# Four-block weight chunks, the residual parked in DRAM, and four seven-product units in every block of gate and up

## The chip, the core and the metric

The kernel runs on one core of one Trainium2 chip. The metric is the device time of one execution in microseconds. TensorE (PE) multiplies, VectorE (DVE) and ScalarE (ACT) prepare its operands, GpSimd (POOL) does a few small operations, and SyncE (SP) issues nearly all loads.

## The reference

One decoder layer for 256 tokens of width 2048, in float32:

```python
f1 = swiglu(rms_norm(h, ffn1_pre_norm), ffn1_w_gate, ffn1_w_up, ffn1_w_down)   # 2048 -> 5504 -> 2048
h = h + 0.5 * rms_norm(f1, ffn1_post_norm)
m = hybrid_token_mixer(rms_norm(h, mix_pre_norm), ...)
h = h + rms_norm(m, mix_post_norm)
f2 = swiglu(rms_norm(h, ffn2_pre_norm), ffn2_w_gate, ffn2_w_up, ffn2_w_down)
h = h + 0.5 * rms_norm(f2, ffn2_post_norm)

def swiglu(x, w_gate, w_up, w_down):
    return (jax.nn.silu(x @ w_gate) * (x @ w_up)) @ w_down
```

The mixer projects its input by `w_in` (2048 to 11280 columns), runs two causal linear attentions with gates (GLA with 4 heads, HGRN2 with 8), multiplies each by a branch matrix, gates and adds the two, and multiplies by `w_out`.

## The kernel before

**Products of split operands.** Each float32 operand is split into a high part (rounded by an ACT copy, `hi`) and a low part (a DVE subtraction, `lo`). A product of two operands is three matmuls (`mm3`, lines 155 to 159): high by high, low by high, high by low. The tokens stand in two tiles of 128 (`t`), and a block of weights has 128 rows and 512 columns (`CB`).

**Plain units and units with seven products.** Gate and up are computed together, one block of 512 columns of each (`gemm_pair`, line 329), into four accumulators `c[t][i]`: two token tiles by two matrices. A unit `u` is two blocks of rows of both matrices, that is four blocks of weights. A plain unit has eight products. A unit with seven products (`Blocks.seven`, line 265, called "a seven" below) uses a Strassen-like scheme: DVE adds blocks of weights to each other, four of the seven products go to shared accumulators `p1`, `p5`, `p6`, `p7`, and three straight to `c`. At the end of the block of columns `share` forms sums of the four and `close` adds them to `c`. It needs sums of the left operand too, made once (`operand_sums`, line 208). `SUMS` gives three units of eight the seven products, `FOUR` gives four. In the FFNs every second block of columns has `FOUR`, and the others have `SUMS`; the first block has none. In the mixer most pairs of columns have `SUMS`. `down_proj` has sevens too, six in each half of its output columns.

**Weights on their way.** SP loads a chunk of two blocks (128x1024 elements) into a `raw` buffer; ACT copies the high part to `whi`; DVE subtracts to get `wlo`. `raw`, `whi` and `wlo` have five buffers each (`RING`). A seven takes two raw buffers and two of each part. The sums of its weights and their high and low parts lie in three tiles of 128x1536 from the pool `rows`, which has three buffers in all (`row_tile`, line 379) that the shared sums and other row tiles use too. A buffer is reused when all that used it before has ended.

**Order.** The order of units in a block of columns is written out in `gemm_pair` (lines 346 to 354). Other work (transposes, attention) is spread between them by `Side`: its `pump` makes a step at each unit. Where `late` is set, in five pairs of columns of the mixer, the sevens come behind the first plain units, with half a plain unit between two sevens, so that attention has the front of the block. The tools that build the program fix the order on each engine beforehand, where an instruction can go ahead of an earlier one that still waits.

**The residual** `h` (2 MB) stays in SBUF through both FFNs; in the mixer it is stored to DRAM (`away`) and its tiles hold other things.

Of the kernel before, what the change touches and what calls it, by code (L numbers as in the profile page):

```python
# [15 lines left out]
P = 128  # L16
# [11 lines left out]
RW = 2 * CB  # L28
STEPS = ((3, 2, 2, 2), (6, 1, 1, 1))
RING = 5  # L30
AHEAD = 3
# [55 lines left out]
def kernel(ctx: ExitStack, tc: tile.TileContext, a: dict, out: bass.AP):  # L87
# [22 lines left out]
    h = [[hpool.tile([P, CB], F32, name=f"h{t}_{n}") for n in range(4)] for t in range(NT)]  # L110

    away = [[dram.tile([P, CB], F32, name=f"away{t}_{n}") for n in range(4)] for t in range(NT)]
# [10 lines left out]

    def ring_alloc(w):
        hi, lo = [ring.tile([P, RW], F32R, tag=s, name=nm(s))[:, :2 * w]
                  .rearrange("p (i c) -> p i c", i=2) for s in ("whi", "wlo")]
        return [(hi, lo)]

    def wload(src: bass.AP, w: int, apart=False):
        raw = ring.tile([P, RW], F32, tag="raw", name=nm("raw"))[:, :2 * w].rearrange(  # L130
            "p (i c) -> p i c", i=2)
        for i in range(2) if apart else [slice(0, 2)]:
            nc.sync.dma_start(raw[:, i, :], src[:, i, :])
        return raw, apart

    def wchunk(src: bass.AP, w: int, alloc=ring_alloc, raw=None):


        raw, apart = raw or wload(src, w)
        parts = alloc(w)  # L140
        if len(parts) == 1:
            hi, lo = parts[0]
            for i in range(2) if apart else [slice(0, 2)]:
                split_into(hi[:, i, :], lo[:, i, :], raw[:, i, :])
            return [(hi[:, i, :], lo[:, i, :]) for i in range(2)]
        for i, (hi, lo) in enumerate(parts):
            split_into(hi, lo, raw[:, i, :])
        return parts
# [12 lines left out]
    def gemm_block(w_dram, c0, w, lhs, nkt=KT, held=None, raws=(), ready=()):  # L161
# [4 lines left out]
        raws, ready = list(raws), list(ready)  # L166
        nb = -(-w // CB)
        step = 2 // nb
        pss = [[ps_tile(f"mm{t}") for _ in range(nb)] for t in range(NT)]

        def chunk(k0, alloc):
            if ready:
                return ready.pop(0)
            raw = raws.pop(0) if raws else None
            src = w_dram[k0 * P:(k0 + step) * P, c0:c0 + w]
            return wchunk(src.rearrange("(k p) c -> p k c", p=P) if nb == 1 else
                          src.rearrange("p (n c) -> p n c", n=nb), w // nb, alloc, raw)

        def mm(t, k0, parts):
            for i, part in enumerate(parts):  # L180
                kt = k0 + i % step
                mm3(pss[t][i // step][:, :w // nb], lhs(t, kt), part, kt == 0, kt == nkt - 1)

        if held is None:
            for k0 in range(0, nkt, step):
                parts = chunk(k0, ring_alloc)
                for t in range(NT):
                    mm(t, k0, parts)
                side.pump()
        else:  # L190
            kept = []
            for i, k0 in enumerate(range(0, nkt, 2)):
                kept.append((k0, chunk(k0, ring_alloc if i < RING else held)))
                mm(0, *kept[-1])
                side.pump()
            for k in kept:
                mm(1, *k)
                side.pump()
            side.flush()
# [45 lines left out]
    class Blocks:  # L245
# [19 lines left out]
        def seven(self, u, end):  # L265
            w, k0 = self.w, 2 * u
            ra, rb = [ring.tile([P, RW], F32, tag="raw", name=nm("raw"))[:, :2 * w]
                      .rearrange("p (i c) -> p i c", i=2) for _ in range(2)]
            wsum, hi, lo = [row_tile(n, d)[:, :, :w] for n, d in
                            (("wsum", F32), ("wsumh", F32R), ("wsuml", F32R))]  # L270

            nc.sync.dma_start(ra[:, 0, :], self.block(0, k0))
            nc.sync.dma_start(ra[:, 1, :], self.block(1, k0 + 1))
            nc.sync.dma_start(rb[:, 0, :], self.block(1, k0))
            nc.sync.dma_start(rb[:, 1, :], self.block(0, k0 + 1))

            (ahi, alo), (bhi, blo) = ring_alloc(w) + ring_alloc(w)
            nc.scalar.activation(ahi, ra, AF.Copy)  # L278
            add(wsum[:, 0:2, :], ra, rb[:, 0:1, :].broadcast_to([P, 2, w]))
            nc.scalar.activation(hi[:, 0:2, :], wsum[:, 0:2, :], AF.Copy)  # L280
            add(rb[:, 0, :], wsum[:, 0, :], ra[:, 1, :])
            nc.scalar.activation(bhi, rb, AF.Copy)  # L282
            summed = add(wsum[:, 2, :], rb[:, 0, :], rb[:, 1, :])
            last[0] = nc.scalar.activation(hi[:, 2, :], wsum[:, 2, :], AF.Copy)  # L284
# [4 lines left out]
            first, second, third = [[(part[0][:, i, :], part[1][:, i, :]) for i in range(n)]  # L289
                                    for part, n in (((ahi, alo), 2), ((bhi, blo), 2), ((hi, lo), 3))]  # L290
# [3 lines left out]
            self.product("p1", self.lhs(0, k0), first[0], end)  # L294
            self.product((0, 1), self.part("s4", u), first[1])
            self.product((0, 0), self.lhs(0, k0 + 1), second[1])
            side.pump()
            self.product("p6", self.part("s2", u), second[0], end)
            self.product("p5", self.part("d", u), third[0], end)
            self.product("p7", self.part("s3", u), third[1], end)  # L300
            self.product((1, 0), self.lhs(1, k0 + 1), third[2])
# [21 lines left out]
    def first_of(w_dram, c0, w=CB):  # L323
        def chunk(i):
            return wchunk(w_dram[2 * i * P:2 * (i + 1) * P, c0:c0 + w]
                          .rearrange("(k p) c -> p k c", p=P), w)
        return chunk

    def gemm_pair(ws, w, lhs, sums, ready=(), following=(), raws=(), sevens=SUMS,
# [11 lines left out]
        def split(i, k0):  # L341
            return wchunk(None, w, raw=raws.pop(0)) if raws else first_of(*ws[i], w)(k0 // 2)

        steps = [(u, i) for u in range(nu) if u not in sevens for i in range(2)]
        if late:
            at = range(6, 6 + 2 * len(sevens), 2)
        elif len(sevens) > len(SUMS):
            at = range(3, 3 + 2 * len(sevens), 2)  # L350
        else:
            at = [2 * u - j for j, u in enumerate(sevens)]
        for j, u in zip(at, sevens):
            steps.insert(j, (u, None))
        ready = list(ready)
        for j, (u, i) in enumerate(steps):
            side.fast = late
            if any(i is None for _, i in steps[j:j + 2]):
                side.full = True
            if i is None:  # L360
# [3 lines left out]
            parts = ready.pop(0) if ready else split(i, k0)  # L364
            if (u, i) == (nu - 1, 0) and sevens:
                ready = [split(1, k0)]
                b.share()
            for t in range(NT):
                b.plain((k0, k0 + 1), t, i, parts, u == nu - 1)
            side.pump()  # L370
        ready = [chunk(0) for chunk in following]
# [162 lines left out]
    def out_proj(w_dram, nkt, lhs, post, scale, pre, homes, following):  # L534
# [8 lines left out]
        def load(kt, hf, alloc=ring_alloc):  # L543
            return wchunk(w_dram[kt * P:(kt + 1) * P, hf * 1024:(hf + 1) * 1024]
                          .rearrange("p (n c) -> p n c", n=2), CB, alloc)

        def mm(t, n, kt, parts):
            if acc[t][n] is None:
                acc[t][n] = ps_tile(f"acc{t}{n}")
            mm3(acc[t][n], lhs(t, kt), parts[n % 2], kt == 0, kt == nkt - 1)  # L550

        order = [(kt, hf) for hf in range(2) for kt in range(2)]
        order += [(kt, hf) for kt in range(2, nkt - TAIL) for hf in range(2)]
        for i, (kt, hf) in enumerate(order):
            parts = load(kt, hf)
            if 6 <= i < 10:
# [5 lines left out]
                load_bcast(wpost[-1], post, i - 6, last[0])  # L562
            for t in range(NT):
                for n in (2 * hf, 2 * hf + 1):
                    mm(t, n, kt, parts)
            if i == 1:
                side.flush()
        tail = [[(kt, load(kt, hf, homes[hf * TAIL + i]))
                 for i, kt in enumerate(range(nkt - TAIL, nkt))] for hf in range(2)]

        for t in range(NT):
            ss = small.tile([P, 4], F32, tag="ss", name=nm("ss"))
            for n in range(4):
                for i, (kt, parts) in enumerate(tail[n // 2]):
# [12 lines left out]
    def down_proj(w_dram, nkt, lhs, sums_of, post, pre, wpost, ys, homes, following):  # L587
# [8 lines left out]
        def split(hf, kt, alloc=ring_alloc):  # L596
            return wchunk(w_dram[kt * P:(kt + 1) * P, hf * 1024:(hf + 1) * 1024]
                          .rearrange("p (n c) -> p n c", n=2), CB, alloc)
# [18 lines left out]
        ahead = []  # L617
        for hf in range(2):
# [6 lines left out]
            kt = 0  # L625
            while kt < n:
                u = kt // 2
# [732 lines left out]
```

## Time and profile before

| | us |
|---|---|
| three runs | 2083.17, 2084.71, 2084.87 (median 2084.71) |
| span of the profiled execution | 2083.3 |
| PE, DVE, ACT, POOL busy | 2069.5, 1855.3, 1240.8, 40.7 |

The profile gives the span of its execution and no time beside it; the median of the runs is 1.4 us above that span. Busy time is counted while at least one instruction of the engine runs; matmuls overlap, so starts say more of their cost than durations do. The first FFN ends near 690 us and the second begins near 1400 us; the mixer lies between.

### The profile page before, as it was taken

How to read it: one execution, taken by the hardware profiler on the slowest of the kernel's cores; microseconds unless marked ns; L12 is line 12 of the kernel's file. 1: busy time of each engine (PE TensorE's matmuls, PEld its weight loads, DVE VectorE, ACT ScalarE, POOL GpSimd, SP SyncE). 2: the span in 40 equal slices, each digit the busy share in tenths (PEclk: the TensorE clock that was granted, in tenths of full speed). 3: DMA queues.
4: the chain of work that ended last, by engine and by line, in shares of the span. 5: the costliest groups of instructions: out<-in, count | busy, mean ns of one | idle time of the engine just before them, and what ended most of it. 6: DMA issues, size and time to landing. Idle time of an engine off the chain costs nothing.

```text
span 2083.3 us, 29324 instructions
## 1 busy us (share of the span) xinstructions
PE 2069.5 (99%) x10509; PEld 1722.0 (83%) x10509; DVE 1855.3 (89%) x2187; ACT 1240.8 (60%) x1670; POOL 40.7 (2%) x87
## 2 busy tenths in 40 slices
PE   9999999999999999999999999999999999999998
PEld 7888888898888888878888888888888888898886
DVE  7898999989899779989999897578999989999896
ACT  6555656566666575576655554465555655666663
POOL 1000000000000100000000000010000000000000
PEclk9999999999999999999999999999999999999999
DMA  8666656667767466555566566755665656576663
GB/s 267 184 209 201 213 187 197 210 185 223 216 191 235 148 201 210 159 172 188 178 195 195 178 220 216 221 182 171 222 197 188 207 187 225 164 238 202 202 206 128
DMA packets 200666, 412.24 MB, mean 198 GB/s; under 512 B 18036, under 2 KB 26423, under 8 KB 200520
## 3 DMA queue, kind: packets, MB, share of 16 engines
q1 hardware_dynamic: 194896, 401.80, 60.9%
q10 hardware_dynamic: 5624, 8.57, 1.4%
q8 instruction: 82, 1.34, 0.3%
q14 instruction: 64, 0.52, 0.1%
HBM read 406.11 MB, written 4.19 MB: 197 GB/s over the span
## 4 chain that ended last, share of the span: by engine, by line
PE 96%; ACT 2%; DVE 1%; issue 1%; DMA 0%; POOL 0%; SPq 0%; DVEq 0%; POOLq 0%; ACTq 0%
PE c L157 22%; PE c L159 21%; PE c L158 21%; PE p L159 5%; PE p L157 5%; PE p L158 5%; PE mm L157 3%; PE mm L159 3%; PE mm L158 3%; PE ps L397 2%; PE acc L157 1%; PE acc L158 1%; PE acc L159 1%; PE ps L905 0%; DVE h L510 0%
## 5 line engine op out<-in xcount | busy, mean ns | idle before, releaser
L151 ACT ACTIVATE whi<-raw 128x1024 fp32r<-128x1024 f32 (+3 forms) x498 | 511.0, 1033 | 284.8 <-PE c L158 116.8
L153 DVE TENSOR_TENSOR wlo<-raw,whi 128x1024 fp32r<-128x1024 f32 (+3 forms) x498 | 587.7, 1190 | 85.5 <-ACT whi L151 84.2
L157 PE MATMUL c<-whi,xhi 128*128 128x512 f32 (+1 forms) x1270 | 495.8, 391 | 0.1
L159 PE MATMUL c<-wlo,xhi 128*128 128x512 f32 (+1 forms) x1270 | 490.9, 387 | 0.0
L158 PE MATMUL c<-whi,xlo 128*128 128x512 f32 (+1 forms) x1270 | 490.6, 386 | 0.0
L243 DVE TENSOR_TENSOR wlo<-raw,whi 128x1024 fp32r<-128x1024 f32 (+1 forms) x252 | 294.5, 1202 | 12.2 <-ACT whi L278 6.1
L159 PEld LDWEIGHTS c<-wlo,xhi 128*128 128x128 f32 x1270 | 238.5, 188 | 47.5 <-DVE wlo L153 0.3
L157 PEld LDWEIGHTS c<-whi,xhi 128*128 128x128 f32 x1270 | 238.6, 188 | 46.3 <-ACT xhi L469 0.5
L158 PEld LDWEIGHTS c<-whi,xlo 128*128 128x128 f32 x1270 | 238.7, 188 | 45.0
L282 ACT ACTIVATE whi<-raw 128x1024 fp32r<-128x1024 f32 (+1 forms) x126 | 131.8, 1046 | 203.9 <-DVE raw L243 80.9
L243 DVE TENSOR_TENSOR wsuml<-wsum,wsumh 128x1536 fp32r<-128x1536 f32 (+1 forms) x126 | 218.1, 1731 | 36.8 <-ACT wsumh L284 36.5
L157 PE MATMUL c<-whi,hkhi 128*128 128x512 f32 x558 | 217.0, 389 | 0.0
L159 PE MATMUL c<-wlo,hkhi 128*128 128x512 f32 x558 | 216.8, 388 | 0.0
L158 PE MATMUL c<-whi,hklo 128*128 128x512 f32 x558 | 216.7, 388 | 0.0
L280 ACT ACTIVATE wsumh<-wsum 128x1024 fp32r<-128x1024 f32 (+1 forms) x126 | 131.6, 1045 | 107.4 <-DVE wsum L243 70.5
L278 ACT ACTIVATE whi<-raw 128x1024 fp32r<-128x1024 f32 (+1 forms) x126 | 131.6, 1044 | 103.0 <-PE c L158 87.7
L243 DVE TENSOR_TENSOR wsum<-raw,raw 128x1024 f32<-128x1024 f32 (+1 forms) x126 | 151.8, 1205 | 21.6 <-DMA raw<-in_ffn_w_down_dram 18.1
L159 PEld LDWEIGHTS c<-wlo,hkhi 128*128 128x128 f32 x558 | 104.7, 188 | 21.6
L158 PEld LDWEIGHTS c<-whi,hklo 128*128 128x128 f32 x558 | 104.7, 188 | 21.4
L157 PEld LDWEIGHTS c<-whi,hkhi 128*128 128x128 f32 x558 | 104.7, 188 | 21.1
L243 DVE TENSOR_TENSOR c<-c,psum 128x512 f32<-128x512 f32 (+1 forms) x135 | 86.5, 683 | 11.8 <-PE c L159 11.4
L243 DVE TENSOR_TENSOR wsum<-raw 128x512 f32<-128x512 f32 (+1 forms) x126 | 86.0, 683 | 3.5
(347 smaller groups left out, 3119.4 us busy)
## 6 DMA issues: line engine op xcount, KB each, us to landing
raw<-in_ffn_w_down_dram SPq DMA_DIRECT2D x124, 512.0 KB, 4.5
raw<-in_w_in_dram SPq DMA_DIRECT2D x104, 512.0 KB, 4.5
raw<-in_ffn_w_up_dram SPq DMA_DIRECT2D x97, 512.0 KB, 4.6
raw<-in_ffn_w_gate_dram SPq DMA_DIRECT2D x96, 512.0 KB, 4.7
raw<-in_ffn_w_gate_dram SPq DMA_DIRECT2D x128, 256.0 KB, 3.7
raw<-in_w_in_dram SPq DMA_DIRECT2D x128, 256.0 KB, 3.5
raw<-in_ffn_w_up_dram SPq DMA_DIRECT2D x126, 256.0 KB, 3.8
raw<-in_ffn_w_down_dram SPq DMA_DIRECT2D x96, 256.0 KB, 4.2
```

The costliest lines, as they stand in the source:

```text
L151: last[0] = nc.scalar.activation(hi, src, AF.Copy)
L153: nc.vector.tensor_tensor(lo, src, hi.bitcast(F32), op=ALU.subtract)
L157: nc.tensor.matmul(ps, lhsT=xhi, rhs=whi, start=start, stop=False)
L158: nc.tensor.matmul(ps, lhsT=xlo, rhs=whi, start=False, stop=False)
L159: nc.tensor.matmul(ps, lhsT=xhi, rhs=wlo, start=False, stop=stop)
L243: return nc.vector.tensor_tensor(o, x, y, op=op)
L278: nc.scalar.activation(ahi, ra, AF.Copy)
L280: nc.scalar.activation(hi[:, 0:2, :], wsum[:, 0:2, :], AF.Copy)
L282: nc.scalar.activation(bhi, rb, AF.Copy)
L397: end = nc.tensor.transpose(dst_ps[:, i * P:(i + 1) * P], src[:, i * P:(i + 1) * P], ident)
```

## The change

- A chunk has four blocks (128x2048). `RW` is doubled; the parts have three buffers (`RING`), the raw chunks two (`RAWS`). In the FFNs the residual's two buffers of 128x2048 serve as two more raw buffers (`roomy`).
- For that the residual is stored to `away2` at the start of the second FFN, and loaded again in the second half of `down_proj` (`residual`): from `x` in the first FFN, from `away2` in the second.
- High and low parts of a chunk are made by one instruction each. `hn` has no tile of its own any more; the SiLU tile is overwritten.
- A seven takes one raw chunk, one buffer of each part, and three row tiles. Two of its four blocks are now loaded into the first row tile, `own`, beside the sum that it holds. The four products of the shared accumulators come first, the three of `c` last.
- Every block of columns of gate and up but the first has four sevens. The order of units is 0, S2, 1, S4, 3, S5, S6, 7 with four, and 0, 1, 3, S2, S4, S6, 5, 7 with three and `late` (S: seven).
- `down_proj` and `out_proj` load chunks of four blocks as well.

```diff
-RW = 2 * CB
+RW = 4 * CB
-RING = 5
-AHEAD = 3
+RING = 3
+RAWS = 2
+AHEAD = 2
...
+    def new_h():
+        for t in range(NT):
+            hrow[t] = hpool.tile([P, 4, CB], F32, tag="hold", name=nm(f"h{t}"), bufs=NT)
+            h[t] = [hrow[t][:, n, :] for n in range(4)]
...
+    def raw_tile(w):
+
+        turn[0] += 1
+        if roomy[0] and turn[0] % (RAWS + NT) >= RAWS:
+            raw = hpool.tile([P, RW], F32, tag="hold", name=nm("raw"), bufs=NT)
+        else:
+            raw = ring.tile([P, RW], F32, tag="raw", name=nm("raw"), bufs=RAWS)
+        return raw[:, :4 * w].rearrange("p (i c) -> p i c", i=4)
...
         def seven(self, u, end):
             w, k0 = self.w, 2 * u
-            ra, rb = [ring.tile([P, RW], F32, tag="raw", name=nm("raw"))[:, :2 * w]
-                      .rearrange("p (i c) -> p i c", i=2) for _ in range(2)]
-            wsum, hi, lo = [row_tile(n, d)[:, :, :w] for n, d in
-                            (("wsum", F32), ("wsumh", F32R), ("wsuml", F32R))]
...
+            raw = raw_tile(w)
+            own, ohi, olo = [row_tile(n, d)[:, :, :w] for n, d in
+                             (("wsum", F32), ("wsumh", F32R), ("wsuml", F32R))]
+
+            load(raw, 1, self.block(0, k0))
+            load(raw, 0, self.block(1, k0))
+            load(own, 0, self.block(1, k0 + 1))
+            load(own, 1, self.block(0, k0 + 1))
+
+            hi, lo = ring_alloc(w)[0]
+            add(raw[:, 2, :], raw[:, 1, :], raw[:, 0, :])
+            nc.scalar.activation(hi[:, 1:3, :], raw[:, 1:3, :], AF.Copy)
+            add(raw[:, 0:4:3, :], raw[:, 0:3:2, :], own[:, 0:1, :].broadcast_to([P, 2, w]))
+            nc.scalar.activation(hi[:, 0:4:3, :], raw[:, 0:4:3, :], AF.Copy)
+            summed = add(own[:, 2, :], raw[:, 3, :], own[:, 1, :])
+            last[0] = nc.scalar.activation(ohi, own, AF.Copy)
             with tc.issue_after(summed.ins):
-                add(alo, ra, ahi.bitcast(F32), ALU.subtract)
-            add(blo, rb, bhi.bitcast(F32), ALU.subtract)
-            add(lo, wsum, hi.bitcast(F32), ALU.subtract)
...
+                add(lo, raw, hi.bitcast(F32), ALU.subtract)
+            add(olo, own, ohi.bitcast(F32), ALU.subtract)
...
+            self.product("p1", self.lhs(0, k0), shared[1], end)
+            self.product("p6", self.part("s2", u), shared[3], end)
+            self.product("p5", self.part("d", u), shared[2], end)
+            self.product("p7", self.part("s3", u), shared[0], end)
             side.pump()
...
+            self.product((0, 1), self.part("s4", u), single[0])
+            self.product((0, 0), self.lhs(0, k0 + 1), single[1])
+            self.product((1, 0), self.lhs(1, k0 + 1), single[2])
...
-        steps = [(u, i) for u in range(nu) if u not in sevens for i in range(2)]
+        steps = [u for u in range(nu) if u not in sevens]
         if late:
-            at = range(6, 6 + 2 * len(sevens), 2)
+            at = range(3, 3 + len(sevens))
         elif len(sevens) > len(SUMS):
-            at = range(3, 3 + 2 * len(sevens), 2)
+            at = (1, 3, 5, 6)
         else:
-            at = [2 * u - j for j, u in enumerate(sevens)]
+            at = sevens
...
                     g, u, ready = gemm_pair(
                         [(a[pre + "_w_gate"], f0), (a[pre + "_w_up"], f0)], w, xl, sums, ready,
                         following, () if f0 else raws,
-                        (FOUR if f0 // CB % 2 == fours else SUMS) if f0 else ())
+                        FOUR if f0 else ())
...
+            def residual():
+                roomy[0] = False
+                new_h()
+                for t in range(NT):
+                    nc.sync.dma_start(hrow[t], a["x"][t * P:(t + 1) * P, :].rearrange(
+                        "p (n c) -> p n c", c=CB) if begin else away2[t])
```

More of the change, by code (lines that the diff above doesn't have):

```diff
@@ L275, in seven @@
[L275 to L283, printed above, removed]
@@ L363, in gemm_pair @@
             k0 = 2 * u
[L364 to L371, printed above, removed]
+            if raws:
+                raw, cuts = raws.pop(0)
+                hi, lo = ring_alloc(w)[0]
+            else:
+                cuts = ()
+                parts = ready or split(load_unit(ws, u, w), w)
+                ready = None
+            if u == nu - 1:
+                if sevens:
+                    b.share()
+            for i in range(2):
+                if cuts:
+                    for c in cuts[i]:
+                        split_into(hi[:, c, :], lo[:, c, :], raw[:, c, :])
+                    parts = [(hi[:, j, :], lo[:, j, :]) for j in range(4)]
+                for t in range(NT):
+                    b.plain((k0, k0 + 1), t, i, parts[2 * i:2 * i + 2], u == nu - 1)
+                side.pump()
+        ready = following and following()
         for i in range(2 if sevens else 0):
@@ L561, in out_proj @@
                 wpost.append(free.pop(0))
[L562 to L569, printed above, removed]
+                load_bcast(wpost[-1], post, kt - 3, last[0])
+            all_of(range(4), (kt, parts))
+        tail = [(kt, chunk(kt, homes[i])) for i, kt in enumerate(range(nkt - TAIL, nkt))]
         for t in range(NT):
@@ L624, in down_proj @@
             units = sorted(DSUMS + DMORE[hf])
-            kt = 0
-            while kt < n:
-                u = kt // 2
-                if kt % 2 == 0 and u + 1 in units and u + 1 not in parts:
+            for kt in range(0, n, 2):
+                u, m = kt // 2, min(2, n - kt)
+                if u + 1 in units and u + 1 not in parts:
                     parts[u + 1] = sums_of(u + 1)
@@ L1164, in mixer @@
             for t in range(NT):
[L1165 to L1167 removed]
+                nc.sync.dma_start(away[t], hrow[t])
+            k, v, ready = two(O_GK, O_GV, None, cols(O_GV + CB, O_GO))
             ks = [scaled(k[t], rs[t], "k") for t in range(NT)]
```

295 lines of the change are left out of this document (158 added, 137 removed).

## The prediction

> **What bounds the kernel now.** I read the page's parts 1 and 4 first: busy time of each engine, and the chain that ended last.
>
> ```profile
> span 2083.3 us, 29324 instructions
> ...
> PE 2069.5 (99%) x10509; PEld 1722.0 (83%) x10509; DVE 1855.3 (89%) x2187; ACT 1240.8 (60%) x1670; POOL 40.7 (2%) x87
> ...
> PE 96%; ACT 2%; DVE 1%; issue 1%; DMA 0%; POOL 0%; SPq 0%; DVEq 0%; POOLq 0%; ACTq 0%
> ```
>
> TensorE is the bound nearly everywhere, so first comes the count of matmuls. How many nanoseconds one costs is read from their starts, since they overlap. Then I cut the first FFN into stretches from one block's transposes to the next block's, and some of the mixer.
>
> ```profile
> 282.96 0.39 PE L159 MATMUL c<-wlo,hkhi 128*128 128x512 f32 x1
> 283.19 0.39 PE L157 MATMUL c<-whi,xhi 128*128 128x512 f32 x1
> 283.41 0.39 PE L158 MATMUL c<-whi,xlo 128*128 128x512 f32 x1
> 283.64 0.39 PE L159 MATMUL c<-wlo,xhi 128*128 128x512 f32 x1
> ...
> 228.49:270.87 42.38, 42.38 (x194) 35.18 (x192) 38.62 (x39) 25.60 (x31) 0.00 (x0) 1.00 0.61 192
> 270.87:312.59 41.72, 41.72 (x190) 34.61 (x189) 39.99 (x41) 23.10 (x28) 0.00 (x0) 1.00 0.66 209
> 752.00:798.00 46.00, 43.54 (x187) 35.57 (x186) 40.09 (x48) 32.36 (x46) 0.00 (x0) 0.96 0.58 183
> 970.00:1015.00 45.00, 45.00 (x447) 36.52 (x446) 44.39 (x72) 28.97 (x47) 0.99 (x2) 1.00 0.55 170
> 1060.00:1110.00 50.00, 50.00 (x407) 40.89 (x405) 49.30 (x82) 26.42 (x31) 1.05 (x2) 1.00 0.64 196
> ```
>
> The columns are length, then busy us of PE, weight load, DVE, ACT and POOL, granted clock, DMA share, GB/s. Starts are 0.68 us apart over three, so a product (three matmuls) costs 0.68, a plain unit (eight products) 5.44, a seven 4.76. The first stretch has three sevens, the second four: 0.66 us less, and PE has no gap in either. But DVE is at 39.99 of 41.72 with four, and at 44.39 of 45.00 and 49.30 of 50.00 in the mixer's blocks with late sevens. DVE stands right behind PE, and any bubble on DVE matters.
>
> **The change, part by part.** *Matmuls.* Ten blocks of gate and up get a fourth seven. Nine are 512 wide: 9 x 0.66 = 5.9. The tenth is 384 wide, and shrinks by the ratio of these two groups: 0.66 x 336/394 = 0.56.
>
> ```profile
> L157 PE MATMUL c<-whi,xhi 128*128 128x512 f32 x1191 | 469.3, 394 | 0.1
> ...
> L157 PE MATMUL c<-whi,xhi 128*128 128x384 f32 x79 | 26.6, 336 | 0.0
> ```
>
> Together -6.5 us.
>
> *Larger instructions.* DVE and ACT do the same elements in fewer instructions.
>
> ```profile
> 228.78 2.35 DVE L243 TENSOR_TENSOR wlo<-raw,whi 128x1024 fp32r<-128x1024 f32 x2
> ```
>
> ```profile
> L243 DVE TENSOR_TENSOR wlo<-raw,whi 128x1024 fp32r<-128x1024 f32 x238 | 281.7, 1217 | 12.2 <-ACT whi L278 6.1 <-ACT whi L282 5.8
> ...
> L243 DVE TENSOR_TENSOR wsuml<-wsum,wsumh 128x1536 fp32r<-128x1536 f32 x119 | 208.6, 1753 | 36.4 <-ACT wsumh L284 36.1
> L243 DVE TENSOR_TENSOR wsum<-raw,raw 128x1024 f32<-128x1024 f32 x119 | 145.1, 1220 | 21.6 <-DMA raw<-in_ffn_w_down_dram 18.1 <-DMA raw<-in_w_in_dram 1.6 <-DMA raw<-in_ffn_w_up_dram 0.6
> L282 ACT ACTIVATE whi<-raw 128x1024 fp32r<-128x1024 f32 x119 | 125.9, 1058 | 194.7 <-DVE raw L243 77.0 <-issue 46.2 <-PE c L159 43.3
> L284 ACT ACTIVATE wsumh<-wsum 128x512 fp32r<-128x512 f32 x119 | 73.5, 618 | 8.0 <-DVE wsum L243 8.0
> ```
>
> Two 1024s take 2.35, so the second adds 1.13 and a start costs about 0.06; an estimate for 2048 is 1.75 + 0.53 = 2.28 alone, 2.2 in a row. Eight merges in a block with four sevens (one in each plain unit and in each seven) give DVE 0.5 us: 39.99 becomes 39.5, below PE's 41.72. That is worth nothing by itself since PE is the bound. It is why the extra sevens fit by sum: 39.5 against 41.72. A wait is not in that sum.
>
> *The wait that is added.* Before, DVE wrote the sums of a seven into a tile of the row pool; nothing was loaded there. Now two blocks are loaded into that tile ("own"). The pool keeps three buffers, and a seven holds all three (own, and the high and low parts, here O and o). So own of the next seven can be issued only after DVE's last subtraction (o) of this one, and O of a seven only after PE has ended the seven before. The limit of three shows already:
>
> ```profile
> ACT wsumh L280 <- PE c L158: 36.2, 39, 7.4
> ...
> DVE wsum L243 <- DMA raw<-in_ffn_w_down_dram: 18.1, 8, 3.9
> ```
>
> ```profile
> DMA to landing us min/median/max: 2.6/3.0/5.2
> ```
>
> (the last: the 256 KB loads of line 274, 100 to 440 us). The load is 3.0 by the median, 2.6 at best, and 5.2 at worst. SP carries the wait in order, and what is queued behind it are the loads of the following units, which have two raw chunks of lead.
>
> *Late blocks of the mixer.* Five pairs of columns are called with late, and there the order becomes 0,1,3,S2,S4,S6,5,7: three sevens without a plain unit between, where a half unit stood between them. From PE's end of S2: O of S4 on ACT 0.44 more than 1.06, so 1.50; o of S4 1.75; own of S6 loads 3.0; the add of two blocks 1.22; their high parts 1.06; the subtraction of four 2.28. That is 10.8. PE wants the low part 4.76 + 0.45 = 5.2 later. The stall is 5.6 (5.2 with a load of 2.6, 7.8 with 5.2). PE can be given something else: unit 5's products of the fourth accumulator, which S6 does not touch, two products or 1.36. Whether the order is arranged so is unknown; instructions do move forward in it, as the seven's first add on DVE did between the closing adds:
>
> ```profile
> 262.41 1.29 DVE L243 TENSOR_TENSOR c<-c,psum 128x512 f32<-128x512 f32 x2
> 263.61 1.21 DVE L243 TENSOR_TENSOR wsum<-raw,raw 128x1024 f32<-128x1024 f32 x1
> 264.74 1.42 DVE L243 TENSOR_TENSOR c<-c,psum 128x512 f32<-128x512 f32 x2
> ```
>
> I take 5.6 - 1.36 = 4.2 in each: 5 x 4.2 = +21. Bounds: 0 (the attention's matmuls fill all of it) to 5 x 7.8 = 39.
>
> *FFN blocks.* The order is 0,S2,1,S4,3,S5,S6,7. The loop from one own to the next is load 3.0, add 1.2, high part 1.06, low part 2.2, o 1.67 and some 0.2 between engines: 9.3. From PE's end of S6, DVE has its share of adds, the closes, the SiLU products and S2:
>
> ```profile
> 304.32 1.21 DVE L243 TENSOR_TENSOR psum<-psum,p 128x1024 f32<-128x1024 f32 x1
> 305.45 2.48 DVE L243 TENSOR_TENSOR c<-c,psum 128x512 f32<-128x512 f32 x4
> 307.85 1.40 DVE L703 SCALAR_TENSOR_TENSOR hn<-c,r,silu 128x512 f32<-128x512 f32 x2
> ```
>
> 1.13 + 2.48 + 1.40 + (1.13 + 0.6 + 2.2 + 1.67 for S2) = 10.6, some 11.4 with waits. Three loops less the last o bring S6's low part to 11.4 + 27.9 - 1.7 = 37.6; 19 matmuls follow (4.3). The block then takes 41.9, against 41.72 of matmuls: 0.2, which unit 7's two free products cover (without that cover, 20 x 0.2 = 4). I take 0. Each 0.1 of load is worth 0.3: at 2.6 nothing waits, at 3.6 it is 43.7, or 2.0 less a cover of 1.36: 0.6 x 20 = +13, and 40 without cover.
>
> By the Trainium skill (DMA: Bandwidth & Descriptors, Anatomy of one DMA) a load has a fixed cost of about 2.0 us, mostly the write's receipt, and moves 436 GB/s beyond that; its fit is for GpSimd's path, these are SP's. An estimate for 256 KB is 2.6, this trace's minimum and not its median. By it the late stall is 5.2 - 1.36 = 3.8, 19 in all, and the sum 2 us lower.
>
> *The rest.* Down: a plain unit stands between sevens, 10.2 of PE against 9.3, and 2.4 more where the sums of the left operand take a row buffer first, or 1.5 behind at about eight places: 0 to +12; I take 0, because split chunks run up to two units (10 us) ahead. Two raw chunks in the mixer instead of five half ones: load 4.6, split 2.0 and 2.3, two in turn, 4.45 a chunk against 5.44: 0 to +5, taken 0.
>
> ```profile
> away<-h SPq DMA_DIRECT2D x8, 256.0 KB, 2.0
> h<-away ACTq DMA_DIRECT2D x8, 256.0 KB, 3.6
> raw<-in_ffn_w_gate_dram SPq DMA_DIRECT2D x96, 512.0 KB, 4.7
> ```
>
> The residual's loads (2 MB in each FFN) and the store stand in SP's queue ahead of weights: hidden by the chunks loaded ahead, else 8 x 3.6 = 29 us of queue in each FFN at worst, of which DMA at 0.66 share has room; I take +1 in all, bounds 0 to +6. The in-place SiLU product and the loads at the start: 0.
>
> Sum: -6.5 + 21 + 0 + 1 = +15.5. The profiled span becomes 2098.8; the runs' median stands 1.4 above the span (2084.71), so 2100.2; say 2100.
>
> **Rivals.**
> (a) *The loads are hidden: faster.* PE gets other work for all of the late stall, or DVE and ACT finish O and o early enough. For it: the mixer's blocks have attention matmuls to move (447 records in 45 us, against 190), and the FFN blocks fit by sum. Against it: O cannot start before PE ends S2, and DVE is 98% busy there. It gives 2084.7 - 6.5 = 2078. It decides when a late block loses less than 6.5/5 = 1.3 us.
> (b) *Stall and saving cancel:* 1 to 2 us in each late block; 2083 to 2088.
> (c) *The FFN's loop binds too:* loads of 3.6 instead of 3.0, under the same traffic of 209 GB/s. +13 to +40 on top: 2113 to 2140. Against it: SP's queue is then emptier than now, and the load is issued alone.
> (d) *The stall slows the clock.* In 752 to 798 PE was idle for 2.5 us and the granted clock was 0.96: 46 x 0.04 = 1.8 us of clock. Five stalls give +9: 2109. The Trainium skill (TensorE: Matmul & The Clock Gate, Part 1) halves the clock after an idle window of about 3.4 us; the row agrees that idling costs clock, and does not show the window.
>
> **How the numbers follow.** The stall in the late blocks as summed has 0.33, (d) 0.10, (c) 0.12, (b) 0.13, (a) 0.32. A measurement of this kernel tells 0.2%, or 4.2 us, from no change. So faster 0.32, same 0.13, slower 0.55. The likeliest one's own range is 2091 (2.4 a block) to 2110 (5.6 a block, and 3 in down). For 8 in 10 the range must reach to (a): 2075, and to the lower half of (c): 2124; what lies beyond is the rest of (c) and a longer load.
>
> **What would show it.** The matmul count falls by 30, and blocks of gate and up are each 41.7 long if the FFN's loop holds. In the mixer's late blocks PE is idle or DVE waits for own, from DMA, once or twice a block, with the load issued right after DVE's subtraction. If PE is at 99% in the mixer as now, (a) is right. A new group in the chain with DMA loads of own in the FFN shows (c); a granted clock under 0.97 in the mixer shows (d). The prediction fails above all if a load of own can get another buffer, or if the free products and attention work are put in the gap.

## The result, and the profile after

The changed kernel takes 2345.38 us (median of four runs, 2345.06 to 2350.11) against 2084.79 before: a ratio of 1.1257, 95% interval 1.1244 to 1.1271. It is slower, as the likeliest case said, but by 260 us and not by 15; the range ended at 2124. The profiled execution spans 2348.2 us.

The page after, parts 1 and 4: busy time, and the chain.

```profile
span 2348.2 us, 27705 instructions
...
PE 2170.8 (92%) x10479; PEld 1744.9 (74%) x10479; DVE 1874.6 (80%) x1852; ACT 1209.4 (52%) x1315; POOL 52.7 (2%) x87
...
PE 3%; DVE 3%; DMA 2%; issue 1%; ACT 1%; POOL 0%; DVEq 0%; SPq 0%; POOLq 0%; ACTq 0%
```

The matmuls fell by 30, as counted. But PE is busy for only 92% of the span, and no engine is full. The chain is of no use here: followed back from the end it explains 10% and then breaks off, so stages and windows take its place. The stages are cut at the first transposes or first matmuls that start each of them:

| stage, us | before | after | sums by DVE | and raw halves |
|---|---|---|---|---|
| to the first block's transposes | 59.7 | 61.3 | 61.1 | 60.1 |
| gate and up, first FFN | 411.4 | 490.7 | 421.8 | 410.5 |
| down, to the first transposes of h | 215.9 | 234.2 | 224.2 | 220.2 |
| to the transposes of k | 111.6 | 113.5 | 114.4 | 110.0 |
| mixer, to the last transposes of sz | 507.9 | 591.3 | 559.8 | 537.0 |
| to the second FFN's first transposes | 135.5 | 136.6 | 136.7 | 135.4 |
| gate and up, second FFN | 410.7 | 481.7 | 421.3 | 408.4 |
| to the end | 230.6 | 238.9 | 235.7 | 230.1 |
| span | 2083.3 | 2348.2 | 2175.0 | 2111.7 |

(The last two columns are experiments, below.) Of the 265 us of span, 150 lie in gate and up, 83 in the mixer, 27 in the two down projections. Two blocks of gate and up and the mixer's stage, as windows, with the columns as in the prediction:

```profile
208.50:259.80 51.30, 46.42 (x190) 36.07 (x189) 40.87 (x34) 24.02 (x21) 0.00 (x0) 0.93 0.50 164
259.80:309.20 49.40, 44.73 (x190) 35.06 (x189) 40.74 (x34) 23.95 (x21) 0.00 (x0) 0.97 0.53 171
899.70:1491.00 591.30, 538.16 (x3328) 427.53 (x3327) 467.23 (x532) 299.83 (x385) 14.77 (x22) 0.96 0.52 165
```

The mixer's stage before, for comparison:

```profile
798.60:1306.50 507.90, 507.48 (x3329) 416.37 (x3328) 465.46 (x620) 306.43 (x472) 14.45 (x22) 1.00 0.61 191
```

A block has the same 190 matmuls as a block with four sevens before, and takes 49.4 to 51.3 us instead of 41.72. PE stands idle for 5 us of it, and its clock is under 1 besides. DVE does 40.9 us of work and idles for 9 to 10: it is not full, it waits. What for shows in DVE's timeline over one block (start, duration, engine, line; in brackets the idle time before and what ended it):

```profile
195.01 2.28 DVE L166 TENSOR_TENSOR wlo<-raw,whi 128x2048 fp32r<-128x2048 f32 x1
...
197.81 2.28 DVE L166 TENSOR_TENSOR wlo<-raw,whi 128x2048 fp32r<-128x2048 f32 x1
...
205.77 1.41 DVE L744 SCALAR_TENSOR_TENSOR silu<-c,r,silu 128x512 f32<-128x512 f32 x2 [1.39 <-ACT silu L775]
...
211.19 2.29 DVE L259 TENSOR_TENSOR wlo<-raw,whi 128x2048 fp32r<-128x2048 f32 x1 [1.68 <-ACT whi L296]
213.40 1.75 DVE L259 TENSOR_TENSOR wsuml<-wsum,wsumh 128x1536 fp32r<-128x1536 f32 x1
...
224.12 1.75 DVE L259 TENSOR_TENSOR wsuml<-wsum,wsumh 128x1536 fp32r<-128x1536 f32 x1
...
230.33 1.23 DVE L259 TENSOR_TENSOR raw<-raw,wsum 128x1024 f32<-128x1024 f32 x1 [1.65 <-DMA wsum<-in_ffn_w_up_dram]
...
232.68 2.29 DVE L259 TENSOR_TENSOR wlo<-raw,whi 128x2048 fp32r<-128x2048 f32 x1 [0.40 <-ACT whi L296]
234.89 1.75 DVE L259 TENSOR_TENSOR wsuml<-wsum,wsumh 128x1536 fp32r<-128x1536 f32 x1
...
240.14 1.23 DVE L259 TENSOR_TENSOR raw<-raw,wsum 128x1024 f32<-128x1024 f32 x1 [1.02 <-DMA wsum<-in_ffn_w_up_dram]
...
244.70 1.75 DVE L259 TENSOR_TENSOR wsuml<-wsum,wsumh 128x1536 fp32r<-128x1536 f32 x1
```

SP's timeline, the loads of own:

```profile
225.90 0.34 SPq L150 DMA_DIRECT2D wsum<-in_ffn_w_up_dram  x1
226.28 0.43 SPq L150 DMA_DIRECT2D wsum<-in_ffn_w_gate_dram  x1
...
236.67 0.33 SPq L150 DMA_DIRECT2D wsum<-in_ffn_w_up_dram  x1
```

This is the loop that the prediction named. The last subtraction of the four sevens (`wsuml`, that is o) ends at 215.15, 225.87, 236.64 and 246.45. SP issues the next load of own 0.03 us after such an end; DVE's add waits for its landing; then the high part, the low part, o. The loops are 10.7, 10.8 and 9.8 us long. The second is 4.46 (o's end to the add) + 1.26 + 1.09 + 2.21 + 1.75. Against the predicted 9.3 only the first number differs by much: 4.46 instead of 3.0. The loads' time to landing, from the page's part 6 (all in us, last column):

```profile
wsum<-in_ffn_w_up_dram SPq DMA_DIRECT2D x72, 256.0 KB, 3.7
wsum<-in_ffn_w_gate_dram SPq DMA_DIRECT2D x72, 256.0 KB, 4.4
```

The fixed cost and rate that the Trainium skill gives (DMA: Bandwidth & Descriptors, Anatomy of one DMA) made an estimate of 2.6 for such a load; the measured 3.7 to 4.4 decide.

The other half of the loss is ahead of the loop. From PE's end of the last seven (198.0) to the first o's end (215.15) are 17.1 us, where the prediction had 11.4: the second of the last plain splits (197.81), thought to fit into a gap before, runs some 2.0 us into this stretch, and two waits of 1.39 and 1.68 us are new. These are 5.1 of the 5.7 us. So 17.1 + 31.3 (three loops) - 1.7 + 4.5 (the matmuls behind) = 51.2: the block.

PE's rows: first the last matmuls of the block before, then the last seven of this one but for its start:

```profile
197.57 0.63 PE L172 MATMUL c<-wsuml,xhi 128*128 128x512 f32 x2
...
238.88 0.40 PE L171 MATMUL c<-whi,xlo 128*128 128x512 f32 x1
242.51 0.79 PE L170 MATMUL p<-whi,hkhi 128*128 128x512 f32 x1 [3.23 <-ACT whi L296]
243.10 0.63 PE L171 MATMUL p<-whi,hklo 128*128 128x512 f32 x1
243.53 0.63 PE L170 MATMUL p<-whi,hkhi 128*128 128x512 f32 x1
...
248.62 0.40 PE L172 MATMUL c<-wsuml,hkhi 128*128 128x512 f32 x1
```

After a stand of 3.23 us the matmuls start 0.43 us apart instead of 0.23, until 248.6: some 6 us at half speed. The Trainium skill (TensorE: Matmul & The Clock Gate, Part 1) has the clock halved after an idle window of about 3.4 us and full again after a busy one of that length; the rows agree in kind, with a stand that is slightly shorter and some 6 us of slow matmuls behind it, and the measurement decides. Gate and up pay this about once a block, the mixer now and then, and the mean granted clock of the whole execution, in the view of the cores, is low:

```profile
core 0: 2348.2 us, clock 0.967
```

That is 2348.2 x 0.033 = 77 us of clock, where 0.998 before made 4. Not all of it is time, since PE would have waited for part of it anyway. In the rows above, 14 matmuls from 242.51 on would have ended near 245.7 at 0.23 each; the next one needs o, which ends at 246.45, and it starts at 248.62. So some 2 us of this block are the clock's (an estimate from these rows). They stand in the last term, the 4.5 us: 12 matmuls follow the end of the low part at 244.78, at 0.23 they would be 2.8 us.

Three lines of the page of waits (total us, times, longest) name the path: load of own, DVE's add, ACT's high part, PE.

```profile
ACT whi L296 <- DVE raw L259: 217.5, 88, 6.2
...
PE p L170 <- ACT whi L296: 94.8, 51, 5.0
DVE raw L259 <- DMA wsum<-in_ffn_w_up_dram: 75.9, 55, 4.2
```

### The profile page after: what moved, and what is told of

It is laid out like the page before. It is cut to its first block, busy times and chain, and to the rows that moved or that the text cites. A ratio compares the mean times of both kernels' runs of the same rounds, so it can differ in the third digit from the quotient of the medians.

```text
span 2348.2 us, 27705 instructions
## 1 busy us (share of the span) xinstructions
PE 2170.8 (92%) x10479; PEld 1744.9 (74%) x10479; DVE 1874.6 (80%) x1852; ACT 1209.4 (52%) x1315; POOL 52.7 (2%) x87
## 5 line engine op out<-in xcount | busy, mean ns | idle before, releaser
L164 ACT ACTIVATE whi<-raw 128x2048 fp32r<-128x2048 f32 (+4 forms) x244 | 448.8, 1845 | 419.2 <-PE c L171 149.7
L166 DVE TENSOR_TENSOR wlo<-raw,whi 128x2048 fp32r<-128x2048 f32 (+4 forms) x244 | 536.2, 2200 | 115.8 <-ACT whi L164 112.9
L170 PE MATMUL c<-whi,xhi 128*128 128x512 f32 (+1 forms) x1088 | 425.2, 391 | 19.1 <-ACT whi L164 19.0
L171 PE MATMUL c<-whi,xlo 128*128 128x512 f32 (+1 forms) x1088 | 421.3, 387 | 0.0
L172 PE MATMUL c<-wlo,xhi 128*128 128x512 f32 (+1 forms) x1088 | 394.6, 389 | 7.0 <-DVE wlo L166 7.0
L259 DVE TENSOR_TENSOR wlo<-raw,whi 128x2048 fp32r<-128x2048 f32 (+1 forms) x136 | 307.3, 2260 | 73.7 <-ACT whi L296 72.1
L259 DVE TENSOR_TENSOR raw<-raw,wsum 128x1024 f32<-128x1024 f32 (+1 forms) x136 | 164.1, 1207 | 129.9 <-DMA wsum<-in_ffn_w_up_dram 75.9
L296 ACT ACTIVATE whi<-raw 128x1024 fp32r<-128x1024 f32 (+1 forms) x136 | 142.3, 1046 | 222.6 <-DVE raw L259 217.5
L298 ACT ACTIVATE wsumh<-wsum 128x1536 fp32r<-128x1536 f32 (+1 forms) x136 | 198.2, 1458 | 10.6 <-DVE wsum L259 7.4
L170 PE MATMUL p<-whi,hkhi 128*128 128x512 f32 (+1 forms) x288 | 124.0, 431 | 79.6 <-ACT whi L296 79.1
L259 DVE TENSOR_TENSOR raw<-raw 128x512 f32<-128x512 f32 (+1 forms) x136 | 92.0, 678 | 51.5 <-DMA raw<-in_ffn_w_up_dram 39.5
L171 PE MATMUL p<-whi,hklo 128*128 128x512 f32 (+1 forms) x288 | 115.5, 411 | 0.0
```

Of the source, the lines that this page charges most:

```text
L164: last[0] = nc.scalar.activation(hi, src, AF.Copy)
L166: nc.vector.tensor_tensor(lo, src, hi.bitcast(F32), op=ALU.subtract)
L170: nc.tensor.matmul(ps, lhsT=xhi, rhs=whi, start=start, stop=False)
L171: nc.tensor.matmul(ps, lhsT=xlo, rhs=whi, start=False, stop=False)
L172: nc.tensor.matmul(ps, lhsT=xhi, rhs=wlo, start=False, stop=stop)
L259: return nc.vector.tensor_tensor(o, x, y, op=op)
```

## The experiments

Theory: (1) the load of own inside the loop from seven to seven is the loss, in FFNs and mixer. Rivals: the fourth seven itself overloads DVE; SP's queue stands behind the waiting load; sevens in a row. When the third run showed that a third of the loss stays without the load, a second part came in: (2) chunks of four in two raw buffers.

**The fourth seven alone, in the kernel before.**

```diff
-                        (FOUR if f0 // CB % 2 == fours else SUMS) if f0 else ())
+                        FOUR if f0 else ())
```

> The kernel before with one part of the change alone: every block of columns of gate and up but the first has four sevens (chunks of two blocks, residual in SBUF as before). If matmuls set the time, ten products of 0.68 us go: 2078, 6 to 7 us less than before. Rival: DVE, at 39.99 of 41.72 us in such a block, can't hold it block after block; then 2084 or more.

Measured: 2078.55 us (seven runs), ratio 0.9973, interval 0.9962 to 0.9984. Two blocks as windows:

```profile
185.50:227.20 41.70, 41.70 (x189) 34.60 (x188) 41.21 (x42) 24.41 (x30) 0.00 (x0) 1.00 0.63 202
227.20:268.90 41.70, 41.70 (x190) 34.62 (x188) 41.08 (x42) 24.43 (x30) 0.00 (x0) 1.00 0.63 202
```

The matmuls' term is right (-6.3 against the 2084.89 measured beside it, for -6.5), and DVE holds four sevens in each block, with half a microsecond to spare (41.2 of 41.70; the 39.99 that the prediction read had pushed some of its work into the neighbours with three). This version beats both kernels, if only by 0.27%. All of the loss comes from the rest of the change.

**After, with three sevens in every second block.**

```diff
-                        FOUR if f0 else ())
+                        (FOUR if f0 // CB % 2 == (0 if begin else 1) else SUMS) if f0 else ())
```

> The changed kernel, but every second block of columns has three sevens again, at their natural places with plain units between. Theory (own's load stands in the loop from seven to seven, about 10.4 us each): the ten blocks with three need 17.1 + 2 x 10.4 - 1.7 + 4.5 = 40.7 us and so come down from 50 to 42.4 to 44: 2265 to 2285 in all. Rival (coarse chunks, three and two buffers, keep PE waiting whatever the sevens do): these blocks stay near 50 and the time above 2320.

Measured: 2300.88 (one run). A block with four, and one with three:

```profile
192.80:244.90 52.10, 46.30 (x190) 35.75 (x189) 41.38 (x34) 24.21 (x21) 0.00 (x0) 0.93 0.49 162
244.90:289.10 44.20, 43.14 (x193) 34.90 (x192) 36.58 (x31) 23.13 (x20) 0.00 (x0) 1.00 0.58 191
```

One turn of the loop less takes 8 us out of a block, nearly as the theory said (42.5 to 44.8 us for 42.4 to 44). It saves less in all, since most blocks with four grew, to 51.4 to 53.0, and the time lies between the two expectations.

**After, without a load in the loop.** All four blocks are loaded into the raw chunk, and DVE writes the sums into the row tile, as before the change; instructions keep their number and sizes. The edit also puts the seven products back into the order of the kernel before, and ACT's first copy no longer waits for an add of DVE (neither is in the excerpt).

```diff
-            load(own, 0, self.block(1, k0 + 1))
-            load(own, 1, self.block(0, k0 + 1))
+            load(raw, 1, self.block(1, k0 + 1))
+            load(raw, 3, self.block(0, k0 + 1))
...
-            add(raw[:, 0:4:3, :], raw[:, 0:3:2, :], own[:, 0:1, :].broadcast_to([P, 2, w]))
+            add(own[:, 0:2, :], raw[:, 0:2, :], raw[:, 2:3, :].broadcast_to([P, 2, w]))
...
```

> The changed kernel, but a seven loads all four blocks into its raw chunk and DVE writes the three sums into the row tile, as before; nothing is loaded into a row buffer. Same number and sizes of DVE, ACT and PE instructions as the changed kernel. Theory (own's load): the loop from seven to seven loses its 4 us of load, blocks of gate and up go from 50 to 42 to 44 us, the granted clock back to 0.99, and the time to 2080 to 2130. Rival (coarse chunks and few buffers): above 2250.

Measured: 2177.28, ratio 1.0449, interval 1.0434 to 1.0463; between the two expectations.

```profile
230.80:274.20 43.40, 42.63 (x190) 34.04 (x189) 40.88 (x34) 24.08 (x22) 0.00 (x0) 1.00 0.62 197
...
821.50:1381.30 559.80, 528.35 (x3328) 421.21 (x3327) 469.29 (x534) 299.72 (x385) 14.70 (x22) 0.98 0.54 175
```

The load in the loop is worth 168 of the 260 us, with the order of the products and the free first copy in that number: this run does not part them from it. A block falls to 43.4 at full clock, with the same work on DVE (40.88). The mixer's stage falls by 31.5. But 92 us stay, of which the mixer has 52.

**After, with the loads of own issued by GpSimd.**

```diff
-            load(own, 0, self.block(1, k0 + 1))
-            load(own, 1, self.block(0, k0 + 1))
+            nc.gpsimd.dma_start(own[:, 0, :], self.block(1, k0 + 1))
+            nc.gpsimd.dma_start(own[:, 1, :], self.block(0, k0 + 1))
```

> The changed kernel, but own's two loads are issued by GpSimd instead of SP, so that a load of own that waits no longer holds back the loads of weights behind it on SP's queue. Theory (the loop through own's load itself): nothing is gained, 2320 to 2380. Rival (SP's queue, weights late behind own): under 2200.

Measured: 2348.69 (one run). Two of these loads in the page's part 6:

```profile
wsum<-in_ffn_w_up_dram POOLq DMA_DIRECT2D x72, 256.0 KB, 3.1
wsum<-in_ffn_w_gate_dram POOLq DMA_DIRECT2D x72, 256.0 KB, 3.4
```

None of them waits in SP's queue there, and the time is the same. So what stands behind the load in SP's queue is not the loss. GpSimd too can issue them only after the same subtraction of DVE, 0.3 us behind it where SP took 0.03. The load is faster, though, and where sevens follow each other the next add starts 3.5 us after o by the median, for 3.9 with SP; gate and up of the first FFN took 13.8 us less, those of the second the same, and the mixer's stage 7 and the last stage 8 more. Why these grew is open.

**After, with the load of own made longer**, by a third block that is loaded and then overwritten.

```diff
             load(own, 1, self.block(0, k0 + 1))
+            load(own, 2, self.block(0, k0 + 1))
```

> The changed kernel with one more load of 256 KB into own ahead of the other two (into the third block, which the sum overwrites later, so the result is the same). Theory (own's load is a link of the loop from seven to seven): own lands 0.6 to 1.0 us later, three loops a block in 20 blocks and the loops of the mixer and of down: 40 to 110 us more, 2385 to 2455. Rival (own's load is hidden, other things bind): under 2360.

Measured: 2440.92 (one run): +95.5, and most blocks of gate and up of 52 to 54.8. The next add starts 4.6 us after o by the median, for 3.9. A longer load makes a longer time: the load is on the path that sets it.

**After, with the mixer's late sevens at their natural places**, and the same in the kernel without the load.

```diff
-            at = range(3, 3 + len(sevens))
+            at = sevens
```

> The changed kernel, but the five late pairs of columns of the mixer have their three sevens at their natural places (0,1,S2,3,S4,5,S6,7) and not one behind the other. Theory (three in a row wait for own's load, 5 to 8 us each pair): 25 to 40 us less than the changed kernel, 2305 to 2320. Rival (the mixer's 83 us come from chunks of four in two raw buffers): within 10 us of 2345.

> The kernel in which DVE writes the sums (2177.3), with the late pairs at natural places as well. Between the transposes of k and those of the last merged gates it still takes 559.8 us against 507.9 before. Theory A (sevens in a row: DVE needs 6.3 us for each against 4.8 of matmuls, and the row buffers come free late): most of the 52 us go, 2130 to 2145. Theory B (two raw chunks in the mixer, loads of 1 MB late): nothing goes, 2165 to 2185.

Measured: 2327.98 and 2183.45 (one run each): 17 us less with the load in the loop, between the two expectations (25 to 40 less, or within 10). Without the load it is 6 more, and the four runs of that kernel without the move reach from 2176.83 to 2181.77: nothing is gained. So three sevens in a row cost some 17 us where own is loaded between them, and they are not what remains in the mixer.

**Two raw chunks of four in the FFNs too** (in the kernel without the load in the loop).

```diff
-                roomy[0] = True
+                roomy[0] = False
```

> The kernel in which DVE writes the sums (2177.3), but the residual's two buffers are not used for raw chunks in the FFNs, so these have two raw chunks as the mixer has; the residual's store and loads stay. Theory A (raw buffers are not what binds): blocks of gate and up stay at 43.4 us, 2175 to 2200 in all. Theory B (two raw chunks are too few): blocks of 45 us and more, 2215 or higher; the mixer's loss would then have the same cause.

Measured: 2301.29 (one run), +124. A block, and the waits of ACT for its chunks:

```profile
247.00:295.50 48.50, 44.84 (x189) 33.67 (x188) 41.26 (x34) 24.02 (x21) 0.00 (x0) 1.00 0.54 174
```

```profile
ACT whi L293 <- DMA raw<-in_ffn_w_up_dram: 111.2, 38, 5.5
...
ACT whi L164 <- DMA raw<-in_ffn_w_up_dram: 79.6, 41, 5.0
```

ACT now stands for loads, and PE behind it. The prediction had put two raw chunks in the mixer at 0 to +5.

**The kernel of the first experiment with four raw buffers of two blocks**, the bytes of two chunks of four (the same edit again in `seven`).

```diff
-        raw = ring.tile([P, RW], F32, tag="raw", name=nm("raw"))[:, :2 * w].rearrange(
+        raw = ring.tile([P, RW], F32, tag="raw", name=nm("raw"), bufs=4)[:, :2 * w].rearrange(
```

> The kernel before with four sevens everywhere (2078.55), but with four raw buffers of two blocks instead of five: eight blocks, as many bytes as two raw chunks of four. Theory A (what the mixer lacks in the changed kernel is lead in bytes): the mixer and the rest lose 20 us or more, above 2098. Theory B (it is the grain: a buffer of four blocks comes free only when all four are split, and its refill of 1 MB then takes 5 us at once): within 6 us, 2075 to 2085.

Measured: 2089.55 (ten runs), ratio 1.0028, interval 1.0018 to 1.0037. Against the five buffers of the first experiment (2078.55) that is 11 us, and none of it lies in the blocks of gate and up, which stay at 41.7, and only 1.3 in the mixer's stage. It is between the two expectations. As many bytes as in two chunks of four cost 11 us in twos here, where going down to two chunks of four had cost 124; the parts differ between these kernels as well. Bytes of lead are a small part of it.

**Raw halves.** In the kernel without the load in the loop, each raw buffer of four blocks (but those that the residual lends) becomes two buffers of two; a chunk is split by two instructions of 1024 columns on each engine. Then the same with no buffers lent in the FFNs.

```diff
-            raw = ring.tile([P, RW], F32, tag="raw", name=nm("raw"), bufs=RAWS)
+            return Halves([ring.tile([P, RW // 2], F32, tag="raw", name=nm("raw"), bufs=2 * RAWS)
+                           [:, :2 * w].rearrange("p (i c) -> p i c", i=2) for _ in range(2)])
...
-            split_into(hi[:, :m, :], lo[:, :m, :], raw[:, at:at + m, :])
+            for b in range(0, m, 2):
+                e = min(b + 2, m)
+                split_into(hi[:, b:e, :], lo[:, b:e, :], raw.at(slice(at + b, at + e)))
```

> The kernel whose sevens get their sums from DVE (2177.28), with each raw buffer of four blocks outside the hold pool made into two buffers of two blocks (the same bytes, four buffers): a chunk is loaded by halves, and split by two ACT copies and two DVE subtractions of two blocks; a half comes free when its own two blocks are split. Parts stay at three buffers of four blocks, and the order is the same. Theory A (the grain of the raw buffers loses the 52 us of the mixer between k and the last sz): that stage falls from 559.8 to 510 to 530, and the time to 2125 to 2150; ACT's waits for raw from w_in fall from 107 us to under 50. Theory B (the large splits, the three parts of four blocks, or the order put out for them lose it): the stage stays at 550 or above, and the time at 2165 or above.

> The same with no further raw buffers in the FFNs (as in the kernel that took 2301.29 with two raw chunks of four, whose blocks of gate and up took 48 to 49.8): four raw buffers of two blocks in all. Theory A (grain of the raw buffers): blocks of gate and up 42 to 44.5, time 2190 or less. Theory B (something else in chunks of four, as the three buffers of the parts, or the bytes of lead): blocks 47 or more, time 2250 or more.

Measured: 2114.70 (ratio 1.0145, interval 1.0116 to 1.0175) instead of 2177.28, and 2148.67 (1.0308, 1.0278 to 1.0338) instead of 2301.29. Windows of the first:

```profile
229.50:271.20 41.70, 41.70 (x190) 34.59 (x189) 41.14 (x42) 24.72 (x26) 0.00 (x0) 1.00 0.61 202
...
800.80:1337.80 537.00, 518.35 (x3328) 419.68 (x3327) 467.92 (x619) 305.83 (x443) 12.66 (x22) 0.99 0.58 181
```

and its waits, ACT's:

```profile
ACT whi L181 <- PE c L188: 117.6, 52, 4.4
ACT whi L313 <- PE c L188: 117.0, 47, 4.3
```

A block of the second, to be held against the 48.50 above:

```profile
275.20:318.40 43.20, 42.07 (x190) 34.57 (x189) 40.85 (x42) 24.07 (x26) 0.00 (x0) 1.00 0.62 195
```

Gate and up are back at 41.7 with DVE nearly full, though the parts still come in chunks of four: the same bytes in twos give back 63 us with four chunks in the FFNs and 153 with two. But the edit does two things at once, and the runs do not part them. A half comes free when its own two blocks are split, where a buffer of four comes free only when the last of its blocks is. And the splits themselves are halved, so that DVE can subtract one half while ACT still copies the other. In the kernel without the load in the loop, with whole splits, DVE waited for ACT before each large subtraction of a seven:

```profile
320.51 2.29 DVE L259 TENSOR_TENSOR wlo<-raw,whi 128x2048 fp32r<-128x2048 f32 x1 [0.98 <-ACT whi L296]
...
329.66 2.29 DVE L259 TENSOR_TENSOR wlo<-raw,whi 128x2048 fp32r<-128x2048 f32 x1 [0.40 <-ACT whi L296]
```

```profile
DVE wlo L259 <- ACT whi L296: 74.1, 111, 4.2
```

With halves 3.9 us of these 74.1 are left. In gate and up of the first FFN no engine waited for a load of raw in the kernel with whole splits, so the 24 us that halves give back in gate and up are more likely the halved splits. With two chunks in the FFNs the loads count: ACT's waits for loads of gate and up are 195 us in all, the longest 5.5, and 154 and 3.8 with halves, while DVE's waits for the second copy (L296 in the one, L316 in the other) fall from 105.5 to 5.6.

In the mixer's stage the halves give back 23 of the 52 us, so the narrower expectation for it (510 to 530) was not met; nor was the one for ACT's waits for w_in, which fell from 107 to 65.5 and not below 50. The last 29 stay open. PE is idle for 18.65 us there, in stands of up to 6 us at attention's transposes and products for most of them, whose order is another than before, and the rest is PE's busy time (518.35 against 507.48), of which the clock of 0.86 between 1250 and 1300 us makes about 7. Whether that order or the parts of four make the stands was not tried.

**The first seven one unit later** (kernel without the load).

```diff
-            at = (1, 3, 5, 6)
+            at = (2, 3, 5, 6)
```

> The kernel in which DVE writes the sums (2177.3), with the order 0,1,S2,S4,3,S5,S6,7 in blocks with four sevens instead of 0,S2,1,S4,3,S5,S6,7. Blocks there take 43.35 us against 41.7 with small chunks, and PE stands still for 1.0 us at the first seven, whose second high part is queued on ACT behind the copies of the transposes. Theory A (the first seven comes too early after the closes): blocks of 41.7 to 42.4 and 2150 to 2165. Theory B (two sevens in a row cost as much wherever they stand): blocks stay at 43 or more, 2170 to 2190.

Measured: 2168.38 (one run), blocks of 42.9: between the two. About a third of the 43.4 - 41.7 lay in the early first seven; raw halves took away all of it, without a move.

Put together: 2345.38 falls by 168.1 without the load in the loop, by 62.6 more with raw halves, and the last 36.2 down to 2078.55 are 29 in the mixer, 4 in down and 3 elsewhere. A fourth row buffer of 6 KB a partition, which would take own's load off the loop directly, was not tried.

## Why the prediction was wrong

- *Matmuls, -6.5:* right; -6.3 by itself. *Larger instructions, 0:* the duration is right (2.28 estimated, 2.28 in the rows above). DVE's load of a block was put at 39.5 and is 40.9: it was read from a block with four sevens between blocks with three, and the neighbours had carried a part.
- *FFN blocks, taken as 0:* the step that failed most, 150 us. The mechanism was there, link by link, and two of its terms were mis-sized: the load (3.0 taken from loads that nobody was waiting for, 3.5 to 4.5 between o and the add), three times a block, 3.4 us; and the start, 11.4 against 17.1, 5.7 us, where the sum counted DVE's own work but not the split and ACT's copies queued in front. Together they are 9.1 of the 9.3 us between 41.9 and 51.2. The last term agrees by luck: 4.3 was meant as 19 matmuls, and 4.5 was 12 of them, most at half speed. A loss of 0.2 us taken as covered by 1.36 left no room for an error of this size in either term.
- *Rival (c)* was this case, at 0.12, and it too was short: it took one term as wrong and kept the others. *Rival (d)* was real in nearly every block of gate and up and not in five places: 77 us of clock, not all of it time, for the 9 us allowed; its sign, a clock under 0.97 in the mixer, came too (0.96). It was set beside (c), but here it follows from the stands that (c)'s loop makes, as the one of 3.23 us above.
- *Late blocks, +21:* supported in kind; 17 us by the run with natural places, and 31.5 in the whole mixer without the load. *Down, 0 (to 12):* 18 and 8, the first above its bound.
- *Two raw chunks in the mixer, 0 (to +5):* failed. The sum compared rates (4.45 us a chunk against 5.44 of PE) as if a buffer were held for its load and split only. It is also held while it waits for ACT and DVE, and is given back whole; buffers and splits of two blocks cost 23 us less in the mixer, and 153 less in the kernel that has two throughout. How much of that is the earlier release alone stays open, as do 29 us of the mixer.
- *Residual, +1:* not measured alone. In the kernel with raw halves, which has it in DRAM too, no stage with its transfers is more than 4.3 us longer than before (down: 220.2 against 215.9), and the others are equal or shorter.
- *Rival (a)* fell: neither the free products nor attention's work filled the gaps (the stand of 3.23 us above, and 538 us of PE in 591 of the mixer).

## What to carry to other kernels

When a load enters a tile of a pool that another step must release first, write down the loop from release to release with the load as it lands under traffic, and hold it against the time of the engine that bounds; a sum that fits by less than the spread of its terms does not fit. Larger chunks at the same bytes are fewer buffers and longer splits: count how many buffers can be in flight while one is still being emptied, and what an engine stands for while the other works on a whole chunk, not the rate. And separate the parts: here the piece that saves (a fourth seven) worked by itself, and two pieces of housekeeping around it cost forty times as much.

## What was not expected of the hardware

The clock: a stand of PE of 3.23 us was followed by some 6 us at half speed, and such stretches, about one in each block of gate and up and some in the mixer, brought the mean clock to 0.967, where the kernel without the load in the loop has 0.991. So a wait can cost again behind its end, some 2 us in the block shown. And the 256 KB loads of own landed in 3.1 and 3.4 us (up, gate) when GpSimd issued them, and in 3.7 and 4.4 from SP; the raw loads of 256 KB of up that SP went on issuing landed in 3.8 instead of 3.0, and the time was the same.
